# A decoder layer with product-key experts on one core: sines earlier, transposes later, expert weights in larger pieces

## The chip, the core and the metric

The kernel runs on 1 core of one Trainium2 chip. That core has TensorE (PE, matrix products into PSUM), VectorE (DVE), ScalarE (ACT), GpSimd (POOL) and SyncE (SP, which here only issues DMAs), and 16 DMA engines that all queues share. The metric is the device time of one execution in microseconds; of several executions the median is taken.

## The reference

One layer over 512 tokens of width 2048, everything in float32:

```python
h = rmsnorm(x, g_mix);  z = h @ w_in                 # 2048 x 4096: pool | q | k | v
x = x + concat(pool_mixer(z), dilated_attention(rope(q), rope(k), v)) @ w_out
x = x + cross_attention(rmsnorm(x), rmsnorm(mem))    # 4 heads, 256 memory tokens
x = x + peer_ffn(rmsnorm(x))                         # see below
out = rmsnorm(x, g_final)

def peer_ffn(h, w_pq, sub_keys_1, sub_keys_2, w_u, w_v):
    # 8 heads: top 16 of 128 keys in each of two halves, then top 16 of their sums
    # -> per token 128 experts out of 16384, with softmax gates
    a = einsum('td,tkd->tk', h, w_u[experts])        # w_u: 16384 x 2048
    return einsum('tk,tkd->td', gates * gelu(a), w_v[experts])
```

## The kernel before

**Tokens.** The 512 tokens are treated in three sets. The first 128 (T0) run ahead of the rest through the whole layer, and their experts are *gathered*: for each of the 128 experts of a token one row of `w_u` (8 KB) is read by an indirect DMA that POOL issues, DVE takes the dot product (`dot0`, L318), and later the same with rows of `w_v` (`axpy0`, L331). One such step moves 128 rows, 1 MB. The next 64 tokens (NS) do the same later (`dot1` L1075, `axpy1` L1086). The remaining 320 tokens (ND) run *dense*: all 16384 experts are multiplied, and gates that are zero for unchosen experts pick the result.

**Exactness.** Products run in the fast float32r form, so each weight tile of 128 x 1024 is split into a high part `wh` (ACT, L143) and a low part `wl` (raw minus high, on DVE or POOL, L144), and each product takes three matmuls (L150 to L152: wh by xh, wh by xl, wl by xh). `load_w` loads a tile (4 KB per partition, 512 KB in all) on SP into a ring of four tiles `wraw`, and splits it into one of three `wh`/`wl` buffers. `lo_eng` says who makes the low part.

**Stages, by the span of the profiled execution.** 0 to 380 us: T0's mixer, attention, cross attention and expert query (`ep` block, matmuls of L399 to L401). 380 to 730: the other 384 tokens' input projection (`z_chunk`, 48 matmuls each) with their attention; the routing of T0 (`pick_steps`: L274, L293, L295, L242 to L246) runs on DVE at the start of it. 730 to 890: output projection. 890 to 1000: cross attention. 1000 to 1140: expert query and its top 16 (`score`). 1140 to 1300: three times, for each block of 128 tokens, `pick` on DVE finds the experts, and three PE transposes (L1054 to L1056) turn the two key indices and the gate; beside it PE computes the first `w_u` chunks (`a_chunk`, 48 matmuls, two weight tiles), seven per block (KB = 7). 1300 to 1690: chunks 21 to 55, with `gates` beside them (L1114, L1116 on DVE, L1119 on PE), which write the dense gates to DRAM; these 56 chunk results are parked in DRAM (`gad`). 1690 to 2700: the mixed stage: 8 groups of 16 `w_v` tiles (`dd`), with the next group's chunk of `w_u` after every even `dd`, so that PE's order of tiles is v, u, u, v, v, u, u, v. 2700 to 3090: `w_v` tiles alone; the chunk results come back from `gad`. Then the final norm.

**What sets the order.** The Python order gives priorities; a planner at build time then orders each engine's instructions by its own simulated timeline, except where an engine is under `manual_schedule`. On the chip every engine works strictly in that order: an instruction that waits holds all behind it. The gathered steps stand in one list, `queue`; `behind(rate)` takes steps off it between matmuls, and `issue_after` keeps each step behind the last low part that DVE made. `RATE` gives the steps per chunk in the stages: z (first three heads' pool chunks differ), output, cross, 1000 to 1300, and 1300 to 1690. In the mixed stage the rate follows from what is left in the list.

The first rope of the second token set needs `sinT` and `cosT`, made by `trig` (L229 to L239) from the positions, which ACT's queue loads at L762.

Of the kernel before, what the change touches and what calls it, by code (L numbers as in the profile page):

```python
# [9 lines left out]
F32 = mybir.dt.float32  # L10
# [24 lines left out]
NS = 64  # L35
SG = P // NS
NK = P // SG
# [3 lines left out]
WRAW = 4  # L41


RATE = (3.0, 2.2, 2.5, 2.0, 0.25, 1.2)
# [19 lines left out]
def hybrid_kernel(ctx: ExitStack, tc: tile.TileContext, a: dict, out: bass.AP):  # L64
# [52 lines left out]
    ring = [None, 0]  # L117

    def load_w2(src):
# [4 lines left out]
        if raw is None:  # L124
            raw = wp.tile([P, 1024], F32, name="wraw", bufs=WRAW)
# [7 lines left out]
    anchor = [None]  # L133

    def load_w(src, lo_eng=None, parts=1):
        raw = wp.tile([P, 1024], F32, name="wraw", bufs=WRAW)
        wh = wp.tile([P, 1024], F32R, name="wh")
        wl = wp.tile([P, 1024], F32R, name="wl")
# [9 lines left out]

    def mm3(ps, wh, wl, xh, xl, start, stop):
# [215 lines left out]
    halo = kt.tile([P, 8, 16], F32, name="halo")  # L365

# [8 lines left out]
    with tc.tile_pool(name="ep", bufs=1) as ep, tc.manual_schedule(engines={mybir.EngineType.SP}):  # L375
# [48 lines left out]
        def mem_in(t):  # L424
            raw = wp.tile([P, 4, MEM], F32, name="wraw", bufs=WRAW)
# [327 lines left out]
    with tc.tile_pool(name="ac", bufs=1, reuse_waits="tile") as ac, tc.tile_pool(name="at", bufs=2, reuse_waits="tile") as at:  # L753
# [116 lines left out]
    with tc.tile_pool(name="xt", bufs=2, reuse_waits="tile") as xt:  # L870
# [78 lines left out]
        for t in range(8):  # L949
            w = load_w(a["w_co"][t], G if t % 2 else V) if t >= 1 else None  # L950
            for e in range(2):
# [9 lines left out]
                sumsq(xtmp, accx, xT[:, c, :], c == 0, TR)  # L961
# [52 lines left out]
    hy = ctx.enter_context(tc.tile_pool(name="hy", bufs=1, side="right", reuse_waits="tile"))  # L1014
# [22 lines left out]
    with tc.tile_pool(name="tw", bufs=1, reuse_waits="tile") as tw:  # L1037
        for b in range(RB):
# [276 lines left out]
```

## Time and profile before

| | |
|---|---|
| time, 3 runs | 3184.94 us median (3177.57 to 3185.37) |
| profiled execution | 3175.37 us, its span 3173.6 us |
| busy | PE 93%, DVE 76%, POOL 45%, ACT 41% of the span |
| granted TensorE clock | 0.968 of full on average |
| DMA | 912.79 MB, 288 GB/s over the span |
| chain that ended last | PE 66%, DVE 20%, DMA 5%, issue 5% |

A busy share is an average over stages that have different limits; the stage table among the rows below shows PE's busy time in each. The granted clock is in parts of full speed: 1.00 is 2.4 GHz and 0.50 is 1.2 GHz; a value between them is a stretch that had both. A wait row reads: who waited, for whom, total us, times, longest.

### The profile page before, as it was taken

How to read it: one execution, taken by the hardware profiler on the slowest of the kernel's cores; microseconds unless marked ns; L12 is line 12 of the kernel's file. 1: busy time of each engine (PE TensorE's matmuls, PEld its weight loads, DVE VectorE, ACT ScalarE, POOL GpSimd, SP SyncE). 2: the span in 40 equal slices, each digit the busy share in tenths (PEclk: the TensorE clock that was granted, in tenths of full speed). 3: DMA queues.
4: the chain of work that ended last, by engine and by line, in shares of the span. 5: the costliest groups of instructions: out<-in, count | busy, mean ns of one | idle time of the engine just before them, and what ended most of it. 6: DMA issues, size and time to landing. Idle time of an engine off the chain costs nothing.

```text
span 3173.6 us, 47405 instructions
## 1 busy us (share of the span) xinstructions
PE 2947.7 (93%) x18311; PEld 2832.5 (89%) x18311; DVE 2422.7 (76%) x3360; ACT 1298.6 (41%) x1789; POOL 1433.8 (45%) x826
## 2 busy tenths in 40 slices
PE   7999879998988997899998999999999999999997
PEld 5868769988978997899998999999999999899997
DVE  7797877798878579599894767777777678787756
ACT  5676534432344443355543333333433333233334
POOL 0000046644534665544546555555555554454532
PEclk9999989999989998999999999999999999999998
DMA  7886737888975344588888989999899999999953
GB/s 261 295 300 214 244 119 282 330 309 339 342 266 192 111 127 124 182 302 318 315 304 315 357 325 359 357 367 355 330 372 353 353 354 358 346 357 362 343 163 106
DMA packets 243521, 912.79 MB, mean 288 GB/s; under 512 B 23488, under 2 KB 85600, under 8 KB 192224
## 3 DMA queue, kind: packets, MB, share of 16 engines
q1 hardware_dynamic: 136304, 471.21, 42.2%
q0 software_dynamic: 55296, 402.68, 32.1%
q10 hardware_dynamic: 51696, 35.88, 3.7%
q8 instruction: 144, 2.36, 0.3%
q14 instruction: 81, 0.66, 0.1%
HBM read 874.22 MB, written 35.45 MB: 287 GB/s over the span
## 4 chain that ended last, share of the span: by engine, by line
PE 66%; DVE 20%; DMA 5%; issue 5%; ACT 2%; POOL 0%; ACTq 0%; POOLq 0%; DVEq 0%; SPq 0%
PE pm L150 11%; PE pm L152 11%; PE pm L151 11%; PE pa L152 9%; PE pa L150 9%; PE pa L151 9%; DVE wl L144 2%; DVE u L1114 2%; DVE oh L295 1%; DVE oh L293 1%; PE pm L400 1%; PE pm L401 1%; PE pm L399 1%; PE pa L1119 1%; DMA rows<-in_w_v_rows_dram,sidx 1%
## 5 line engine op out<-in xcount | busy, mean ns | idle before, releaser
L144 POOL TENSOR_TENSOR wl<-wraw,wh 128x1024 fp32r<-128x1024 f32 x369 | 930.5, 2526 | 1433.3 <-ACT wh L143 1401.4
L143 ACT ACTIVATE wh<-wraw 128x1024 fp32r<-128x1024 f32 (+1 forms) x658 | 693.7, 1058 | 1042.1 <-PE pm L151 467.0
L152 PE MATMUL pa<-ch,wl 128*128 128x320 f32 x2048 | 634.5, 312 | 25.4 <-DVE wl L144 23.5
L150 PE MATMUL pm<-dH,wh 128*128 128x320 f32 x2048 | 640.4, 313 | 15.0 <-DVE cl L1164 6.5
L152 PE MATMUL pm<-dH,wl 128*128 128x320 f32 x2048 | 640.6, 313 | 6.1 <-DVE wl L144 3.9
L150 PE MATMUL pa<-ch,wh 128*128 128x320 f32 x2048 | 636.7, 311 | 7.3 <-DVE xT L1193 4.7
L151 PE MATMUL pm<-dL,wh 128*128 128x320 f32 x2048 | 639.0, 312 | 0.0
L151 PE MATMUL pa<-cl,wh 128*128 128x320 f32 x2048 | 635.3, 310 | 0.0
L144 DVE TENSOR_TENSOR wl<-wraw,wh 128x1024 fp32r<-128x1024 f32 (+1 forms) x289 | 377.4, 1308 | 166.5 <-ACT wh L143 158.7
L152 PEld LDWEIGHTS pa<-ch,wl 128*128 128x128 f32 x2048 | 387.1, 189 | 30.4 <-DVE wl L144 28.1
L150 PEld LDWEIGHTS pm<-dH,wh 128*128 128x128 f32 x2048 | 389.2, 190 | 16.3 <-DVE cl L1164 6.8
L150 PEld LDWEIGHTS pa<-ch,wh 128*128 128x128 f32 x2048 | 388.3, 190 | 10.2 <-ACT ch L1163 5.2
L152 PEld LDWEIGHTS pm<-dH,wl 128*128 128x128 f32 x2048 | 389.3, 190 | 8.2 <-DVE wl L144 5.4
L151 PEld LDWEIGHTS pm<-dL,wh 128*128 128x128 f32 x2048 | 389.3, 190 | 0.0
L151 PEld LDWEIGHTS pa<-cl,wh 128*128 128x128 f32 x2048 | 388.1, 190 | 0.0
L150 PE MATMUL pm<-hH,wh 128*128 128x384 f32 x1024 | 355.9, 348 | 10.4 <-DVE k L811 3.4
L152 PE MATMUL pm<-hH,wl 128*128 128x384 f32 x1024 | 354.2, 347 | 10.5 <-DVE wl L144 10.5
L151 PE MATMUL pm<-hL,wh 128*128 128x384 f32 x1024 | 354.4, 346 | 5.2 <-DVE hL L874 4.4
L1193 DVE TENSOR_TENSOR xT<-pa,xT 128x320 f32<-128x320 f32 x256 | 124.7, 487 | 196.6 <-PE pa L152 191.0
L150 PEld LDWEIGHTS pm<-hH,wh 128*128 128x128 f32 x1024 | 197.6, 193 | 17.1 <-issue 5.8
L152 PEld LDWEIGHTS pm<-hH,wl 128*128 128x128 f32 x1024 | 197.6, 193 | 13.4 <-DVE wl L144 12.5
L151 PEld LDWEIGHTS pm<-hL,wh 128*128 128x128 f32 x1024 | 197.7, 193 | 6.9 <-DVE hL L874 4.7
(413 smaller groups left out, 4571.6 us busy)
## 6 DMA issues: line engine op xcount, KB each, us to landing
wraw<-in_w_u_dram SPq DMA_DIRECT2D x256, 512.0 KB
wraw<-in_w_v_dram SPq DMA_DIRECT2D x256, 512.0 KB
wraw<-in_w_in_dram SPq DMA_DIRECT2D x64, 512.0 KB
xT<-in_w_in_f_dram SPq DMA_DIRECT2D x63, 512.0 KB
gd<-stage SPq DMA_DIRECT2D x10, 2048.0 KB
gt<-gd ACTq DMA_DIRECT2D x32, 640.0 KB
wraw<-in_w_pq_f_dram SPq DMA_DIRECT2D x32, 512.0 KB
wraw<-in_w_out_dram SPq DMA_DIRECT2D x32, 512.0 KB
```

The source lines that it names most:

```text
L143: S.activation(wh[:, c], raw[:, c], AF.Copy)
L144: i = (lo_eng or V).tensor_tensor(wl[:, c], raw[:, c], wh.bitcast(F32)[:, c], op=ALU.subtract)
L150: TE.matmul(ps, wh, xh, start=start, stop=False)
L151: TE.matmul(ps, wh, xl, start=False, stop=False)
L152: TE.matmul(ps, wl, xh, start=False, stop=stop)
L293: V.tensor_tensor(oh, iota50.unsqueeze(1).broadcast_to([P, 16, NCAND]), cf[:, h, :].unsqueeze(2).broadcast_to([P, 16, NCAND]), op=ALU.is_e ...
L295: V.tensor_tensor(oh, oh, ecand[:, h, :].unsqueeze(1).broadcast_to([P, 16, NCAND]), op=ALU.mult)
L399: TE.matmul(ps, xh, wh, start=start, stop=False)
L400: TE.matmul(ps, xh, wl, start=False, stop=False)
L401: TE.matmul(ps, xl, wh, start=False, stop=stop)
L1114: V.tensor_tensor(u, iota.unsqueeze(1).unsqueeze(1).broadcast_to([P, 2, 4, P]), e12T[:, :, t:t + 4].unsqueeze(3).broadcast_to([P, 2, 4, P] ...
L1193: V.tensor_tensor(xT[:, dd, NS:], ps[:, :ND], xT[:, dd, NS:], op=ALU.add)
```

## The change

1. `trig` for the second token set moves from the attention block into the block before (hooks of the expert query of T0); its tables are kept in `accx` and in a new `cosT`.
2. The three transposes after each `pick` stand behind the seven chunks of their block in the program, and `issue_after(last_mm)` keeps them behind the last matmul of those chunks.
3. In the mixed stage each `w_u` chunk's low parts go to POOL for the first tile and DVE for the second, where they went to one engine for both, changing from chunk to chunk. With `w_v`, whose even tiles go to DVE and odd ones to POOL, the two now take strict turns.
4. `w_u` and `w_v` are laid out so that one DMA brings two tiles, 8 KB per partition, 1 MB; `load_pair` puts them in a ring of three pairs: two in the old four tiles, the third in `xraw`, where the token rows `htok` lay. Those rows go to DRAM (`hyd`) and are read back when the 64 tokens' steps begin; their result stays in a row buffer.
5. `RATE` rises in the early stages and falls in the stage of 1300 to 1690 (1.2 to 0.95). The sum of squares beside the last cross projection adds on POOL. The 64 tokens' normed rows take one DVE instruction where they took two.

```diff
-RATE = (3.0, 2.2, 2.5, 2.0, 0.25, 1.2)
+RATE = (3.2, 2.4, 2.8, 2.5, 0.25, 0.95)
...
+    wraw = wp.tile([P, 4, 1024], F32, name="wraw", bufs=1)
+    slot = [0, 0]
+
+    def raw1():
+        slot[0] += 1
+        return wraw[:, slot[0] % 4]
+
+    def load_pair(src):
+        slot[1] += 1
+        i = slot[1] % 3
+        raw = xraw if i == 2 else wraw[:, 2 * i:2 * i + 2]
+        nc.sync.dma_start(raw, src)
+        return raw
...
-        TE.matmul(ps, wl, xh, start=False, stop=stop)
+        last_mm[0] = TE.matmul(ps, wl, xh, start=False, stop=stop)
...
-            V.tensor_tensor(acc, acc, q, op=ALU.add)
+            (eng or V).tensor_tensor(acc, acc, q, op=ALU.add)
...
+        def trig_rows():
+            V.tensor_copy(cosT, posr[0])
+            V.tensor_scalar(cosT, cosT, scalar1=invf, scalar2=None, op0=ALU.mult)
+            trig(cosT, ep.tile([P, TR], F32, name="jk", bufs=2)[:32], sinT, cosT)
+            V.tensor_scalar(sinT[0:16], sinT[0:16], scalar1=-1.0, scalar2=None, op0=ALU.mult)
+
+        hooks_x[2][0] = [pos_in]
+        hooks_x[2][5] = [trig_rows]
...
-        posi = tmp2k(TR, I32)[:32]
-        nc.scalar.dma_start(posi, a["positions"][:, T0:].broadcast_to([32, TR]))
-        ang = tmp2k()[:32]
-        V.tensor_copy(ang, posi)
-        V.tensor_scalar(ang, ang, scalar1=invf, scalar2=None, op0=ALU.mult)
-        trig(ang, tmp2k()[:32], sinT, cosT)
-        V.tensor_scalar(sinT[0:16], sinT[0:16], scalar1=-1.0, scalar2=None, op0=ALU.mult)
...
-                sumsq(xtmp, accx, xT[:, c, :], c == 0, TR)
+                sumsq(xtmp, accx, xT[:, c, :], c == 0, TR, eng=G)
...
-        lo = G if j < RB * KB else (V, G) if j < K1 else G if j < K1 + GRP or j % 2 == 0 else V
-        ps = proj_one(a["w_u"][j], dH, dL, ND, lo_eng=lo, rate=RATE[4] if j < RB * KB else RATE[5] if j < K1 else 0)
+        lo = G if j < RB * KB else (V, G) if j < K1 else G if j < K1 + GRP else (G, V)
+        ps = proj_one(None, dH, dL, ND, raw=load_pair(a["w_u"][j]), lo_eng=lo, rate=RATE[4] if j < RB * KB else RATE[5] if j < K1 else 0)
...
+            a_until(KB * b + KB)
             pt = pa.tile([P, 512], F32, name="pa")
-            TE.transpose(pt[:, 0:P], e12[:, 0, :], ident)
-            TE.transpose(pt[:, P:2 * P], e12[:, 1, :], ident)
-            TE.transpose(pt[:, 2 * P:3 * P], gtf, ident)
+            with tc.issue_after(last_mm[0].ins):
+                TE.transpose(pt[:, 0:P], e12[:, 0, :], ident)
+                TE.transpose(pt[:, P:2 * P], e12[:, 1, :], ident)
+                TE.transpose(pt[:, 2 * P:3 * P], gtf, ident)
...
-            a_until(KB * b + KB)
...
-    def start1():
+    def start1(s):
         gx[0] = gxp.tile([P, D], F32, name="gx")
-        S.copy(gx[0], hy1)
+        r = row_tile()
+        nc.sync.dma_start(r, hyd[s])
+        S.copy(gx[0], r)
...
-                wh, wl = load_w(a["w_v"][g, dd], lo_eng=G if dd % 2 else V)
+                if dd % 2 == 0:
+                    vraw = load_pair(a["w_v"][g, dd // 2])
+                wh, wl = load_w(None, lo_eng=G if dd % 2 else V, raw=vraw[:, dd % 2])
...
-    A["w_u"] = np.ascontiguousarray(i["w_u"][0].reshape(P, NCH, 2, 8, P).transpose(1, 2, 4, 3, 0)).reshape(NCH, 2, P, 1024)
+    A["w_u"] = np.ascontiguousarray(i["w_u"][0].reshape(P, NCH, 2, 8, P).transpose(1, 4, 2, 3, 0)).reshape(NCH, P, 2, 1024)
```

Three places show what the planner makes of it. ACT between the second and the third routing of a block (1252 to 1290 us before): `gT` is the copy that follows each group of transposes, `wh` a split weight tile, `ga` the result of one chunk. Before, from the second `gT` to the third:

```order
L1060 COPY gT<-pa 128x128
L301 ACT_TABLE_LOAD
L301 ACTIVATE gt<-gt 128x128
L143 ACTIVATE wh<-wraw 128x1024 x2
L1026 ACT_TABLE_LOAD
L1026 ACTIVATE ga<-pm 128x320
L143 ACTIVATE wh<-wraw 128x1024 x2
L1026 ACTIVATE ga<-pm 128x320
L143 ACTIVATE wh<-wraw 128x1024 x2
L1026 ACTIVATE ga<-pm 128x320
L143 ACTIVATE wh<-wraw 128x1024
L1060 COPY gT<-pa 128x128
```

Now, the last twelve rows up to the third `gT`:

```order
L160 ACTIVATE wh<-wraw 128x1024
L160 ACTIVATE wh<-xraw 128x1024
L1051 ACTIVATE ga<-pm 128x320
L160 ACTIVATE wh<-xraw 128x1024
L160 ACTIVATE wh<-wraw 128x1024
L1051 ACTIVATE ga<-pm 128x320
L160 ACTIVATE wh<-wraw 128x1024 x2
L1051 ACTIVATE ga<-pm 128x320
L160 ACTIVATE wh<-wraw 128x1024
L160 ACTIVATE wh<-xraw 128x1024
L1051 ACTIVATE ga<-pm 128x320
L1088 COPY gT<-pa 128x128
```

Three chunk results stood between the two copies, and seven do now (three of them above these rows). On PE the three groups of transposes stood behind 410, 578 and 761 of the chunks' matmuls, and stand behind 394, 672 and 1008.

DVE at the first head of the attention (386 to 392 us before): `k` is the first key, t2k the buffers of `trig` and of the rope's shuffle. Before, `trig` (L764 to L239) begins between the top-16 instructions:

```order
L811 TENSOR_TENSOR k<-ma,r2c 128x384
L245 MAX mb<-ma 128x8
L246 MAX_INDEX mb<-mb,ma 128x8
L764 CAST t2k<-t2k 32x384
L246 MAX_INDEX mb<-mb,ma 128x8
L244 MATCH_REPLACE ma<-mb,ma 128x128
L765 TENSOR_SCALAR t2k<-t2k,invf 32x384
L244 MATCH_REPLACE ma<-mb,ma 128x128
L245 MAX mb<-ma 128x8
L229 TENSOR_SCALAR t2k<-t2k 32x384
L773 STREAM_SHUFFLE t2k<-q 32x384
```

Now both shuffles of the rope follow the key at once:

```order
L835 TENSOR_TENSOR k<-ma,r2c 128x384
L264 MAX mb<-ma 128x8
L265 MAX_INDEX mb<-mb,ma 128x8
L797 STREAM_SHUFFLE t2k<-q 32x384
L797 STREAM_SHUFFLE t2k<-k 32x384
```

The instructions of `trig` are gone from here; the first of them now stands among the splits of T0's cross-attention input, 173 rows ahead of this `k`, and the last after the third group of T0's expert query.

SP in the mixed stage, with the engines whose semaphores each load waits for. Before, one row is one tile:

```order
L142 DMA wraw<-in_w_v_dram 128x1024 [waits DMAHW6_49,Pool_49]
L142 DMA wraw<-in_w_v_dram 128x1024 [waits DMAHW7_49,DVE_49]
L142 DMA wraw<-in_w_u_dram 128x1024 [waits DMAHW0_49,DVE_49]
L142 DMA wraw<-in_w_u_dram 128x1024 [waits DMAHW1_49,DVE_49]
L142 DMA wraw<-in_w_v_dram 128x1024 [waits DMAHW2_49,Pool_49]
```

Now one row is two tiles:

```order
L129 DMA wraw<-in_w_u_dram 128x2048 [waits DMAHW4_49,Pool_49]
L129 DMA wraw<-in_w_v_dram 128x2048 [waits DMAHW2_49,DVE_49,Pool_49]
L129 DMA xraw<-in_w_u_dram 128x2048 [waits DMAHW7_49,Pool_49]
L129 DMA xraw<-in_w_v_dram 128x2048 [waits DMAHW4_49,DVE_49,Pool_49]
L129 DMA wraw<-in_w_u_dram 128x2048 [waits DMAHW6_49,DMAHW1_49,Pool_49]
```

A `w_u` pair now waits for POOL's low part of the second tile of the `w_v` pair three loads back, whose place it takes; a `w_v` pair takes the place of a `w_u` pair.

## Rows read from the trace of the kernel before

**Rows 1.** The windows view, by stage; busy us (instructions) per engine, PEclk, DMA share, GB/s.
```profile
380.00:520.00 140.00, 117.66 (x627) 111.22 (x628) 102.19 (x262) 53.07 (x95) 64.76 (x45) 0.88 0.44 150
520.00:730.00 210.00, 195.22 (x1045) 182.62 (x1044) 178.86 (x228) 77.51 (x141) 118.22 (x87) 0.96 0.88 328
730.00:890.00 160.00, 150.19 (x821) 148.25 (x820) 130.35 (x138) 53.62 (x71) 81.98 (x53) 0.97 0.88 338
890.00:1000.00 110.00, 91.74 (x449) 81.59 (x448) 86.34 (x119) 53.73 (x104) 38.84 (x27) 0.91 0.63 230
1140.00:1300.00 160.00, 128.52 (x810) 126.03 (x809) 153.03 (x381) 52.09 (x67) 93.17 (x36) 0.88 0.39 123
1300.00:1690.00 390.00, 371.45 (x2626) 366.83 (x2625) 327.43 (x282) 187.02 (x209) 195.37 (x91) 0.98 0.82 301
1690.00:2700.00 1010.00, 992.17 (x6708) 989.54 (x6707) 720.03 (x689) 356.69 (x438) 545.19 (x326) 0.99 0.92 351
2700.00:3090.00 390.00, 366.07 (x2415) 359.63 (x2414) 285.48 (x299) 126.17 (x150) 183.21 (x104) 0.98 0.86 316
```

**Rows 2.** The waits view, PE, 380 to 520: total us, times, longest.
```profile
PE pa L818 <- POOL q L776: 13.3, 1, 13.3
```

**Rows 3.** The windows view in slices of 10 us, the first head.
```profile
400.00:410.00 10.00, 0.00 (x0) 0.00 (x0) 10.00 (x62) 3.16 (x4) 3.55 (x4) 0.68 0.10 30
410.00:420.00 10.00, 4.67 (x12) 2.78 (x12) 9.97 (x33) 0.83 (x2) 2.58 (x3) 0.50 0.11 43
```

**Rows 4.** The timeline of DVE, 375 to 420: start, us, [idle before <-releaser].
```profile
389.96 0.35 DVE L764 CAST t2k<-t2k 32x384 f32<-32x384 int32 x1 [2.95 <-DMA t2k<-in_positions_dram]
```

**Rows 5.** The waits view, PE, 1000 to 1300.
```profile
PE pa L1054 <- DVE e L1052: 20.8, 3, 11.0
```

**Rows 6.** One line, L1054: number, duration ns min/median/max, first and last start.
```profile
L1054 PE MATMUL pa<-ident,e x3: 448/474/476, 1212.4 to 1289.7; 128*128 128x128 f32 x3
```

**Rows 7.** The timeline of PE, 1238 to 1256.
```profile
1252.09 0.47 PE L1054 MATMUL pa<-ident,e 128*128 128x128 f32 x1 [10.96 <-DVE e L1052]
```

**Rows 8.** The windows view in slices of 20 us, after the third routing.
```profile
1300.00:1320.00 20.00, 20.00 (x138) 20.00 (x137) 0.00 (x0) 7.33 (x9) 14.51 (x7) 1.00 0.60 193
```

**Rows 9.** The windows view in slices of 100 us, one where PE never waits.
```profile
2000.00:2100.00 100.00, 100.00 (x684) 100.00 (x683) 70.24 (x61) 36.21 (x44) 55.59 (x34) 1.00 0.93 349
```

**Rows 10.** Groups by line, DVE: count, busy us, mean ns, idle before.
```profile
L318 DVE CUSTOM_DVE_ANT_0 rows<-rows,gx 128x2048 f32<-128x2048 f32 x66 | 150.0, 2276 | 6.4 <-DMA rows<-in_w_u_rows_dram,sidx 6.4
L225 DVE TENSOR_TENSOR accx<-accx,xtmp 128x384 f32<-128x384 f32 x30 | 19.8, 659 | 1.9 <-ACT xtmp L224 1.8
```

**Rows 11.** Groups by line, POOL and ACT (part 5 of the page for L144, L143).
```profile
L144 POOL TENSOR_TENSOR wl<-wraw,wh 128x1024 fp32r<-128x1024 f32 x369 | 930.5, 2526 | 1433.3 <-ACT wh L143 1401.4
L143 ACT ACTIVATE wh<-wraw 128x1024 fp32r<-128x1024 f32 (+1 forms) x658 | 693.7, 1058 | 1042.1 <-PE pm L151 467.0
L1003 POOL TENSOR_TENSOR qh<-xT,r2c 128x320 f32<-128x320 f32 x16 | 13.9, 879 | 0.0
```

**Rows 12.** DMA queues, 2105 to 2106 us: packets, MB, share of 16 engines.
```profile
q0 software_dynamic: 38, 0.29, 67.9%
q1 hardware_dynamic: 39, 0.13, 32.2%
```

**Rows 13.** DMA queues, 2285 to 2286 us, the rows of 8 KB read by ACT.
```profile
q10 hardware_dynamic: 49, 0.40, 100.8%
```

**Rows 14.** The timeline of SP, 2285 to 2310.
```profile
2293.60 1.42 SPq L142 DMA_DIRECT2D wraw<-in_w_v_dram  x2
```

**Rows 15.** The timeline of ACT, 2262 to 2312.
```profile
2305.35 1.06 ACT L143 ACTIVATE wh<-wraw 128x1024 fp32r<-128x1024 f32 x1 [4.53 <-DMA wraw<-in_w_v_dram]
```

**Rows 16.** The waits view, all engines, 1690 to 2700.
```profile
PE pa L152 <- DVE wl L144: 8.1, 4, 3.0
```

**Rows 17.** The waits view, all engines, 2700 to 3090.
```profile
PE pa L152 <- DVE wl L144: 15.4, 13, 2.3
ACT wh L143 <- DMA wraw<-in_w_v_dram: 16.2, 6, 4.5
```

More of the change, by code (lines that the diff above doesn't have):

```diff
@@ L34 @@
 RB = TR // P
-NS = 64
-SG = P // NS
-NK = P // SG
+SETS = ((0, 64),)
+NS = sum(n for _, n in SETS)
 ND = TR - NS
 NTB = ND // 32
-WRAW = 4
-RATE = (3.0, 2.2, 2.5, 2.0, 0.25, 1.2)
+RATE = (3.2, 2.4, 2.8, 2.5, 0.25, 0.95)
 PK, Z0 = 3, 1
@@ L133, in hybrid_kernel, with split_tiles, load_w @@
     anchor = [None]
[L135 to L138, printed above, removed]
+    def split_tiles():
+        return wp.tile([P, 1024], F32R, name="wh"), wp.tile([P, 1024], F32R, name="wl")
+    def load_w(src, lo_eng=None, parts=1, raw=None):
+        there = raw is not None
+        raw = raw if there else raw1()
+        wh, wl = split_tiles()
         n = 1024 // parts
@@ L141, in load_w @@
             c = slice(p_ * n, (p_ + 1) * n)
-            nc.sync.dma_start(raw[:, c], src[:, c])
+            if not there:
+                nc.sync.dma_start(raw[:, c], src[:, c])
             S.activation(wh[:, c], raw[:, c], AF.Copy)
@@ L1086, in axpy1, with end1 @@
         V.scalar_tensor_tensor(out=gx[0], in0=r, scalar=sact2[:, k:k + 1], in1=gx[0], op0=ALU.mult, op1=ALU.add)
-    def end1():
-        y1[0] = hy.tile([P, D], F32, name="htok")
-        S.copy(y1[0], gx[0])
-    queue += [start1] + [lambda k=k: dot1(k) for k in range(NK)] + [turn1] + [lambda k=k: axpy1(k) for k in range(NK)] + [end1]
-    with tc.tile_pool(name="gw", bufs=2, side="right", reuse_waits="tile") as gw:
+    def end1(s):
+        ys[s] = row_tile()
+        S.copy(ys[s], gx[0])
@@ L1095, in hybrid_kernel, with add1 @@
+    def add1(s):
+        o, n = SETS[s]
         for k4 in range(4):
             pt = pa.tile([P, 512], F32, name="pa")
-            for kk in range(4):
-                k = 4 * k4 + kk
-                hn = gw.tile([P, SG, NS], F32, name="hn0")
-                for g in range(SG):
-                    V.scalar_tensor_tensor(out=hn[:, g, :], in0=xT[:, k, :NS], scalar=gains[:, 3, k:k + 1], in1=r2c[:, :NS], op0=ALU.mult, op1=ALU.mult)
-                TE.transpose(pt[:, kk * P:(kk + 1) * P], hn.rearrange("p g t -> p (g t)"), ident)
@@ L1103, in hybrid_kernel @@
-            S.copy(hy1[:, k4 * 512:(k4 + 1) * 512], pt)
+            with tc.issue_after(last_mm[0].ins):
+                for kk in range(4):
+                    TE.transpose(pt[:, kk * P:(kk + 1) * P], ys[s][:, (4 * k4 + kk) * P:(4 * k4 + kk + 1) * P], ident)
+            x = xT[:, 4 * k4:4 * k4 + 4, o:o + n]
+            for g in range(P // n):
+                V.tensor_tensor(x, pt.rearrange("p (k g t) -> p k g t", k=4, t=n)[:, :, g, :], x, op=ALU.add)
+    for s, (o, n) in enumerate(SETS):
+        ks, at_ = range(o, o + n), len(queue) + 6
+        queue += [lambda s=s: start1(s)] + [lambda k=k: dot1(k) for k in ks] + [lambda c=slice(o, o + n): turn1(c)]
+        queue += [lambda k=k: axpy1(k) for k in ks] + [lambda s=s: end1(s)]
+        if s:
+            queue.insert(at_, lambda s=s - 1: add1(s))
@@ new lines, in hybrid_kernel @@
+    with tc.tile_pool(name="gw", bufs=2, side="right", reuse_waits="tile") as gw:
+        for s, (o, n) in enumerate(SETS):
+            for k4 in range(4):
+                pt = pa.tile([P, 512], F32, name="pa")
+                for kk in range(4):
+                    k = 4 * k4 + kk
+                    hn = gw.tile([P, P // n, n], F32, name="hn0")
+                    V.scalar_tensor_tensor(out=hn, in0=xT[:, k, o:o + n].unsqueeze(1).broadcast_to([P, P // n, n]), scalar=gains[:, 3, k:k + 1],
+                                           in1=r2c[:, o:o + n].unsqueeze(1).broadcast_to([P, P // n, n]), op0=ALU.mult, op1=ALU.mult)
+                    TE.transpose(pt[:, kk * P:(kk + 1) * P], hn.rearrange("p g t -> p (g t)"), ident)
+                hs4 = gw.tile([P, 512], F32, name="hs4")
+                S.copy(hs4, pt)
+                nc.scalar.dma_start(hyd[s, :, k4 * 512:(k4 + 1) * 512], hs4)
@@ L1203, in hybrid_kernel @@
                 behind(1000)
-                for k4 in range(4):
-                    pt = pa.tile([P, 512], F32, name="pa")
-                    for kk in range(4):
-                        TE.transpose(pt[:, kk * P:(kk + 1) * P], y1[0][:, (4 * k4 + kk) * P:(4 * k4 + kk + 1) * P], ident)
-                    o = xT[:, 4 * k4:4 * k4 + 4, :NS]
-                    for sg_ in range(SG):
-                        V.tensor_tensor(o, pt.rearrange("p (k g t) -> p k g t", k=4, t=NS)[:, :, sg_, :], o, op=ALU.add)
+                add1(len(SETS) - 1)
                 for k in range(KD):
```

51 lines of the change are left out of this document (29 added, 22 removed).

## The prediction

> **What bounds the kernel now.** I read the table by stage first [rows 1]. PE is the wall: in the mixed stage (1690 to 2700 us) it is busy 992 of 1010 us, and a slice in which it never waits holds 684 matmuls in 100 us, 0.146 us each [rows 9]. A tile of 24 matmuls therefore takes 3.5 us. So time can come only from PE's idle stretches and from the low clock behind them. The largest, as a share, lie at the first head (380 to 520: 22 us idle, clock 0.88) and in the routing (1140 to 1300: 31 us idle, clock 0.88, with DVE busy 153 of 160). Between 1300 and 1690 PE idles 19 us, in the last `w_v` stage 24, in the whole mixed stage 18 [rows 1]. The waits view then names what PE waits for: the rope's sines in one wait of 13.3 us [rows 2] and the routing's transposes in three waits of 20.8 us [rows 5]. Of the weights it names only low parts that come late, 8.1 and 15.4 us [rows 16, 17].
>
> **Early sines.** DVE's cast of the positions waited 2.95 us for the DMA and started at 389.96 [rows 4]; the rest of `trig` followed between top-16 steps, and PE stood from 398 to 412. Its next slices hold 0 and 4.67 us of work, at clock 0.68 and 0.50 [rows 2, 3]. With the tables made long before, rope can follow the key at once, and PE loses neither the 13.3 us nor all of the slow clock behind them. The wait that is next is DVE, which is full in both slices [rows 3]: T0's routing is still there, and the scores' softmax queues in it. At worst all 13.3 us return as that wait (gain 0); at best the idle and slow time of both slices goes (about 15 idle, 22 with the clock). I take 15 of gain, near the upper end, since the order now has both shuffles ahead of the routing's large steps. `trig` itself, about ten DVE instructions of at most 0.5 us and two of ACT, goes to a stretch in which DVE is busy but PE also waits: cost 0 to 6, I take 2.
>
> **Later transposes.** Before, PE reached them at 1212.4, 1252.1 and 1289.7 [rows 6, 7], behind 410, 578 and 761 chunk matmuls, and waited each time. DVE's routing sets these times and is not changed. Now they stand behind 394, 672 and 1008. From 1212.4 on, 278 matmuls take 41 us, to 1253: the second routing is ready. Then 336 take 49 us, to about 1303 with the transposes: the third has been ready for 13 us. Before, at 1303 PE had done 761 + 13.5/0.146, about 851. The difference of 157 matmuls is 23 us. POOL makes these low parts, 2.53 us per tile of 3.5 [rows 11], so it keeps up. Ends: 0 if DVE takes it all back in the gates behind, 31 (the whole idle). I take 23, because DVE lies idle from 1300 to 1320 [rows 8]: it waits for PE's chunk 21 there, and gets it earlier now.
>
> **Rates.** Steps moved forward: z 11 x 0.2 + 8 x 0.2 = 3.8, output 16 x 0.3 = 4.8, cross 4 x 0.5 = 2; taken from 1300 to 1690: 35 x 0.25, about 9. A step costs DVE 2.28 us [rows 10]. So DVE loses 20 us of work where it is busy 327 of 390, and gains 9, 11 and 5 us where it has 31, 30 and 24 idle [rows 1]. I cost the forward steps at a third, 8, and the relief at half, 11: gain 3. If every forward step stalls PE half its length, loss 13; if the relief is worth 12 and the rest is free, gain 12.
>
> **Small edits.** The sums of squares leave DVE (15 x 0.66 = 10 us) for POOL (879 ns for 320 columns, so about 1.05 us for 384, 16 us) [rows 10, 11]; POOL is busy 39 of 110 there [rows 1]. Gain 2, ends -5 and 5. The first `xraw` load waits until PE has read the last tile of the pool that it replaces, and SP's next loads wait behind it; chunk 0 covers it with 7 us. Cost 2, ends 0 and 5. The 64 tokens' steps begin with a 1 MB read of `hyd`, issued by SP a few loads ahead; if late, DVE and with it PE wait. Cost 2, ends 0 and 8.
>
> **The ring of three pairs.** Where `w_u` or `w_v` comes alone, the ring is deeper than four tiles: the sixteen microseconds of waits for `w_v` loads after 2700 [rows 17] should go. PE waits there for DVE's low parts, whose DVE work the change leaves; gain 5, ends -8 and 15. In the mixed stage it is the reverse. PE's order is v u u v, 14.0 us a turn. A `w_u` pair takes the place of the `w_v` pair before, whose second tile is split only after both `w_u` tiles of its turn. From the landing of one `w_u` pair: ACT copies 1.06 us, POOL makes its first low part, then that of the next odd `w_v` tile, 2.53 each [rows 11]; then SP may issue the next pair: 6.1 us, or about 7.2 if POOL issues a row gather in between. This leaves 6.8 to 7.9 us from issue to landing before the turn grows. What does 1 MB take? With the gathers active, both queues moved about equal packets, 38 and 39 in one microsecond, but 0.29 MB of rows of 8 KB against 0.13 MB of weights of 4 KB [rows 12]. The engines take turns by packet. A load that ACT issued in 8 KB pieces moved 49 packets with 0.40 MB [rows 13], so pieces of 8 KB stay whole, and the weights' share rises from a third to half: about 0.2 MB/us, 5 us, and 2.5 us where no gather runs. No row shows alone what comes ahead of the first packet and behind the last: I add an estimate of 1 to 3 us, since the 11.7 us [rows 14, 15] are more than 0.52 MB takes at 0.13. So 4 to 8 us, against 6.8 to 7.9: mostly in time, with nearly none of the old slack. The worst of before took about 11.7 us from issue to split [rows 14, 15]. Against it, strict turns end POOL's three low parts in a row, part of the 8.1 us [rows 16]. Ends: gain 8, or 64 turns (8 groups of 8) x 1.1 us = 70. I take a cost of 10, nearer the low end, since the steady rows give in-time loads.
>
> The Trainium skill, page DMA: Bandwidth & Descriptors, section Anatomy of one DMA, fits a DMA by 2.0 us plus its bytes over 436 GB/s: 4.4 us for 1 MB, and the ring would cost 0, the sum -42. The trace differs: half that size took 11.7 us at worst here [rows 14, 15], so I keep 10.
>
> **Sum.** -15 + 2 - 23 - 3 - 2 + 2 + 2 - 5 + 10 = -32 us, against the profiled execution's 3175.37 (span 3173.6): 3143. That execution lay 9.6 us under the median of the runs, 3184.94, and I put the same sum on the median: 3153.
>
> **Rivals.**
> *The pairs come late (slower).* If the first-served rows and the start of each load keep a `w_u` pair 8 us or more on the way, each mixed turn grows. At 1.0 us a turn it costs 64; the other terms give -42, so +22: 3207. It decides from 0.66 us a turn. For it: the 11.7 us [rows 14, 15] and DMA at 0.92 busy [rows 1]. Against: equal packets [rows 12] and slack where no gather runs. It would be sure if the 8 KB pieces went as two packets of 4 KB: the share stays a third, 1 MB takes 1/0.14 = 7.1 us plus 1 to 3, and 0.2 to 3 us a turn are lost. The Trainium skill, same page, section SWDGE vs HWDGE vs iDMA, says that a packet is preferably at most 4096 B; by this rule that would happen, but the trace disagrees, with 49 packets for 0.40 MB [rows 13].
> *The routing's gain is given back.* If DVE's gates end no earlier, the 23 us return as PE's wait on them: -9, 3176. For it: DVE's 327 of 390 [rows 1]. Against: its idle slice [rows 8].
> *Everything gains.* Ring -4 instead of +10, last stage -12, rates -9: -59, 3126. For it: PE's waits on late low parts [rows 16, 17]; against: DVE's load is unchanged there.
>
> **Chances.** The forecast 0.47 (its own range 3130 to 3176), late pairs 0.20, gain given back 0.19, everything gains 0.14. The three runs spread by 8 us, and 0.3% (9.6 us) is what a measurement can tell from no change: faster means below 3175, slower above 3194. Faster: 0.44 + 0.14 + 0.07 = 0.65. Same: 0.03 + 0.04 + 0.10 = 0.17. Slower: 0.16 + 0.02 = 0.18. The range from 3115 to 3200 leaves out the worse half of the late pairs and the best of the last case.
>
> **What would show it.** In the new profile: PE's wait on POOL's rope at the first head under 3 us, and no empty slice there; transposes 15 us earlier by the sines, the first at about 1197 with its wait, the third at about 1288 with none; 1690 reached some 40 us earlier; the mixed stage 1010 to 1030 us long, with ACT waiting for `w_u` loads more than for `w_v`; `w_v` waits gone after it. Wrong, if the mixed stage is longer by over 40 us (late pairs), or if the start of the mixed stage moves by less than 20 us.

## The result and the profile after

The changed kernel takes 3420.21 us (3415.48 to 3425.57), the one before 3181.26 beside it: ratio 1.0752, 95% interval 1.0725 to 1.0779. It is slower by some 239 us, where 28 to 32 us of gain were forecast, and lies 220 us above the range. Where the time went is read first from the stages. Two rows of the view by line give marks: the first and the last start of the `w_u` products (`pm<-dH`) and of the `w_v` products (`pa<-ch`). Before:

```profile
L150 PE MATMUL pm<-dH,wh x2048: 304/309/636, 1136.8 to 2653.4; 128*128 128x320 f32 x187
L150 PE MATMUL pa<-ch,wh x2048: 304/308/607, 1740.9 to 3150.7; 128*128 128x320 f32 x187
```

After:

```profile
L169 PE MATMUL pm<-dH,wh x2048: 305/309/636, 1150.2 to 2862.6; 128*128 128x320 f32 x187
L169 PE MATMUL pa<-ch,wh x2048: 307/310/636, 1738.7 to 3391.1; 128*128 128x320 f32 x187
```

From these, four stages: up to the first chunk 1136.8 us before, 1150.2 after (+13); chunks 0 to 55 took 604.1, now 588.5 (-16); the mixed stage 912.5, now 1123.9 (**+211**); the last stage 497.3, now 528.5 (+31). The windows view of the profile after has in the same stretches as [rows 1]:

```profile
380.00:520.00 140.00, 123.04 (x669) 116.29 (x669) 110.25 (x259) 52.94 (x96) 75.62 (x52) 0.90 0.49 176
1140.00:1300.00 160.00, 129.17 (x831) 126.40 (x830) 152.96 (x409) 54.84 (x73) 98.53 (x39) 0.91 0.39 130
1300.00:1690.00 390.00, 376.42 (x2689) 372.40 (x2687) 320.29 (x260) 187.75 (x213) 191.56 (x83) 1.00 0.78 286
1690.00:2700.00 1010.00, 886.70 (x5554) 855.32 (x5555) 650.55 (x539) 291.52 (x362) 483.33 (x270) 0.95 0.73 286
2700.00:3090.00 390.00, 344.19 (x2159) 332.37 (x2158) 275.23 (x281) 113.12 (x142) 177.29 (x103) 0.95 0.82 312
```

From 1690 to 2700 PE had 6708 matmuls and now has 5554; the clock fell from 0.99 to 0.95, and the DMA engines are busy 0.73 where they were 0.92. So over the stage bandwidth is not what is short. Between the marks of the mixed stage PE is busy 982 us for some 6120 matmuls, before 903 for as many, and waits 142 us, before 9: of the 211 us, 133 are waits and 78 busy time, with the clock at 0.95 where it was 0.99. What PE waits for there, 1690 to 2862:

```profile
PE pm L169 <- ACT wh L160: 51.4, 38, 3.3
PE pa L169 <- ACT wh L160: 43.2, 34, 1.3
PE pm L171 <- POOL wl L161: 41.4, 29, 1.9
PE pm L169 <- DVE cl L1212: 7.7, 1, 7.7
```

High parts are late, where [rows 16] had only low parts, and ACT makes them late because it waits for `w_u` loads. The loop stands in one turn. SP, the issues of pairs:

```profile
2090.70 0.33 SPq L129 DMA_DIRECT2D wraw<-in_w_v_dram  x1
2095.16 0.33 SPq L129 DMA_DIRECT2D wraw<-in_w_u_dram  x1
2109.17 0.33 SPq L129 DMA_DIRECT2D wraw<-in_w_v_dram  x1
2112.36 0.33 SPq L129 DMA_DIRECT2D xraw<-in_w_u_dram  x1
```

ACT, the high parts of the same turn (a bracket gives the idle time before and its releaser):

```profile
2104.52 2.00 ACT L160 ACTIVATE wh<-wraw 128x1024 fp32r<-128x1024 f32 x2 [6.45 <-DMA wraw<-in_w_u_dram]
2106.43 1.04 ACT L160 ACTIVATE wh<-xraw 128x1024 fp32r<-128x1024 f32 x1
2122.57 2.01 ACT L160 ACTIVATE wh<-xraw 128x1024 fp32r<-128x1024 f32 x2 [1.03 <-DMA xraw<-in_w_u_dram]
```

POOL, from the landing of that `w_u` pair to the release of the next place:

```profile
2105.65 2.36 POOL L161 TENSOR_TENSOR wl<-wraw,wh 128x1024 fp32r<-128x1024 f32 x1 [8.60 <-ACT wh L160]
2108.16 1.75 POOL L114 DMA_INDIRECT rows<-in_w_v_rows_dram,sidx  x1 [0.15 <-issue]
2109.94 2.39 POOL L161 TENSOR_TENSOR wl<-xraw,wh 128x1024 fp32r<-128x1024 f32 x1
```

The pair issued at 2095.16 lands at 2104.52. High part, low part, a row gather and the low part of the second `w_v` tile take until 2112.33, 7.8 us; at 2112.36 SP issues the next `w_u` pair, and it lands at 2122.57, 10.2 us later. Over the some 60 turns in which ACT waited for the load, landing to next issue has a mean of 8.3 us (7.9 where POOL issues one row gather in that time, 9.1 where it issues two) and issue to landing one of 9.3; together 17.6, and a turn takes 1123.9/64 = 17.6 where it took 14.3. SP has mostly issued a `w_v` pair 3 to 4.5 us ahead of the `w_u` pair, here at 2090.70 and 2109.17. From the issue at 2095.16 to the landing at 2104.52 the queues (q0 the gathers, q1 the loads of SP) moved:

```profile
q0 software_dynamic: 387, 2.91, 73.6%
q1 hardware_dynamic: 146, 1.06, 26.9%
```

The 1.06 MB are the `w_u` pair itself: the `w_v` pair had moved its bytes by then, and the gathers moved 2.91 MB beside it. Summed in this way over the turns, the gathers move 2.4 MB on average between issue and landing, and the `w_v` pair 0.25 MB. Counted back from the landing by the pair's own bytes, the 9.3 us are 3.3 up to its first packets, 4.6 while it moves, and 1.4 from there to its use. The first half of the prediction's reading stands (packets stay whole, half of the bytes [rows 12, 13]): 1 MB in 4.6 us is about its 0.2 MB/us. What stands ahead of the first packet and behind the last took longer than it said.

### The profile page after: what moved, and what is told of

Read it like the earlier page. It is cut to its first block, busy times and chain, and to the rows that moved or that the text cites. A ratio compares the mean times of both kernels' runs of the same rounds, so it can differ in the third digit from the quotient of the medians.

```text
span 3413.7 us, 46891 instructions
## 1 busy us (share of the span) xinstructions
PE 3026.6 (89%) x18311; PEld 2869.6 (84%) x18311; DVE 2518.2 (74%) x3329; ACT 1292.8 (38%) x1790; POOL 1490.6 (44%) x841
## 3 DMA queue, kind: packets, MB, share of 16 engines
q8 instruction: 144, 2.36, 0.3%
## 5 line engine op out<-in xcount | busy, mean ns | idle before, releaser
L161 POOL TENSOR_TENSOR wl<-wraw,wh 128x1024 fp32r<-128x1024 f32 x275 | 691.3, 2516 | 1235.8 <-ACT wh L160 1175.3
L160 ACT ACTIVATE wh<-wraw 128x1024 fp32r<-128x1024 f32 (+1 forms) x488 | 506.7, 1054 | 913.1 <-PE pm L170 310.7
L169 PE MATMUL pm<-dH,wh 128*128 128x320 f32 x2048 | 662.0, 323 | 85.7 <-ACT wh L160 64.7
L171 PE MATMUL pm<-dH,wl 128*128 128x320 f32 x2048 | 662.5, 324 | 52.3 <-POOL wl L161 48.8
L170 PE MATMUL pm<-dL,wh 128*128 128x320 f32 x2048 | 655.5, 320 | 1.0 <-DVE dL L236 1.0
L169 PEld LDWEIGHTS pm<-dH,wh 128*128 128x128 f32 x2048 | 405.2, 198 | 98.7 <-ACT wh L160 80.7
L161 DVE TENSOR_TENSOR wl<-wraw,wh 128x1024 fp32r<-128x1024 f32 (+1 forms) x213 | 335.5, 1575 | 187.4 <-ACT wh L160 184.1
L170 PEld LDWEIGHTS pm<-dL,wh 128*128 128x128 f32 x2048 | 404.0, 197 | 1.3 <-DVE dL L236 1.2
L161 POOL TENSOR_TENSOR wl<-xraw,wh 128x1024 fp32r<-128x1024 f32 x94 | 238.3, 2537 | 318.7 <-ACT wh L160 307.6
L160 ACT ACTIVATE wh<-xraw 128x1024 fp32r<-128x1024 f32 x170 | 176.9, 1055 | 303.6 <-DMA xraw<-in_w_u_dram 87.4
```

What stands on the lines that cost most here:

```text
L171: last_mm[0] = TE.matmul(ps, wl, xh, start=False, stop=stop)
```

## The experiments

e1 to e4, e8, e13 and e14 are edits of the kernel after, e5 to e7 and e9 to e12 of the kernel before. Stages in us by the marks above (in the order u u v v, marked *, the border between mixed and last shifts, so only their sum compares); ratios to the kernel before, run on the same chip, with 95% intervals. Each stage is of one execution. Of an edit only the deciding lines are shown, some shortened and with comments added.

| kernel | to 1st chunk | chunks | mixed | last | median | ratio |
|---|---|---|---|---|---|---|
| before | 1136.8 | 604.1 | 912.5 | 497.3 | 3175 to 3182 | |
| after | 1150.2 | 588.5 | 1123.9 | 528.5 | 3420.21 | 1.0752 (1.0725 to 1.0779) |
| e1 tiles | 1154.1 | 597.7 | 934.3 | 524.2 | 3232.15 | 1.0150 (1.0111 to 1.0189) |
| e2 no turns | 1151.4 | 587.3 | 1056.6 | 525.1 | 3344.99 | 1.0531 (1.0490 to 1.0573) |
| e3 u u v v | 1148.0 | 595.7 | 902.7* | 540.9* | 3214.04 | 1.0112 (1.0080 to 1.0144) |
| e4 four pairs | 1149.3 | 585.6 | 944.2 | 537.7 | 3239.71 | 1.0190 (1.0154 to 1.0225) |
| e5 rates | 1148.6 | 591.8 | 939.5 | 517.2 | 3225.50 | 1.0151 (1.0136 to 1.0165) |
| e6 transposes | 1134.5 | 596.6 | 913.4 | 504.2 | 3164.19 | 0.9959 (0.9943 to 0.9974) |
| e7 sines | 1116.5 | 606.0 | 910.4 | 503.0 | 3164.54 | 0.9968 (0.9952 to 0.9984) |
| e8 u u v v, old rates | 1128.2 | 608.9 | 910.6* | 519.2* | 3191.29 | 1.0041 (1.0026 to 1.0057) |
| e9 sines, transposes | 1121.3 | 598.4 | 912.2 | 497.5 | 3151.68 | 0.9922 (0.9903 to 0.9941) |
| e10 last rate | 1136.7 | 592.6 | 936.2 | 512.9 | 3203.25 | 1.0086 (1.0066 to 1.0106) |
| e11 early rates | 1150.7 | 586.8 | 927.3 | 494.5 | 3184.18 | 1.0025 (1.0011 to 1.0040) |
| e12 strict turns | 1135.2 | 605.8 | 940.9 | 522.9 | 3225.97 | 1.0149 (1.0127 to 1.0172) |
| e13 w_u first | 1148.9 | 587.6 | 990.6 | 537.1 | 3291.12 | 1.0355 (1.0334 to 1.0376) |
| e14 w_u first, plain | 1131.5 | 608.2 | 948.2 | 524.8 | 3237.39 | 1.0188 (1.0159 to 1.0217) |

**The ring of pairs.** e1 releases tile by tile:

```diff
-        i = slot[1] % 3
-        raw = xraw if i == 2 else wraw[:, 2 * i:2 * i + 2]
+        i = slot[1] % 6          # one tile, 512 KB, per DMA
+        raw = xraw[:, i - 4] if i > 3 else wraw[:, i]
```

> The kernel after, with the same memory and the same DRAM layout, but as a ring of six single tiles: each tile is loaded by its own DMA (4 KB per partition, 512 KB) when its own slot is free. Theory L (the turn is a loop: a w_u pair may be issued only after POOL's low part of the second w_v tile of the turn before, and then lies about 10 us behind the w_v pair issued 3 us ahead of it): the turn falls from 17.5 to 14.0-14.3 us, total 3190 to 3225 us. Theory P (1 MB pieces of 8 KB are slow in themselves): the same here, 3190 to 3225. Theory T (the strict turns hold POOL): no change of the turn, 3390 to 3440.

e2 undoes the strict turns:

```diff
-G if j < K1 + GRP else (G, V)
+G if j < K1 + GRP or j % 2 == 0 else V
```

> The kernel after, with the strict turns undone: in the mixed stage a w_u chunk's two low parts go to one engine, changing from chunk to chunk. Theory T (POOL's two low parts and a gather in a row delay the release of the place): the turn falls by 2 us or more, total 3200 to 3300. Theory L: on POOL's chunks the loop grows by one low part of 2.5 us, on DVE's it shrinks by as much, mean the same, total 3380 to 3440. Theory P: 3400 to 3440.

e3 puts the chunk ahead of the even tile:

```diff
                 if dd % 2 == 0:
+                    if not last:
+                        nxt.append(c_chunk(GRP * order[i + 1] + dd // 2))
                     vraw = load_pair(a["w_v"][g, dd // 2])
...
-                if dd % 2 == 0 and not last:
-                    nxt.append(c_chunk(GRP * order[i + 1] + dd // 2))
```

> The kernel after, with pairs and their ring as they are, but PE's order in the mixed stage u u v v instead of v u u v (the chunk stands ahead of the even w_v tile), so that places come free in the order in which they were filled. Theory L: the released place has a whole pair of 7 us in reserve, the turn falls to 14.0-14.6 us, total 3190 to 3240. Theory P: the loads stay late, 3350 to 3430. Theory T: 3380 to 3440.

e4 has a fourth pair:

```diff
-        i = slot[1] % 3
+        i = slot[1] % 4          # i == 3: xraw2, in the place of rowx
```

> The kernel after, with a ring of four pairs, the fourth in the place of one of the four buffers of the gathered rows. Theory L: a w_u pair takes the place of a w_u pair, which is free half a turn earlier; the turn falls to 14.0-14.5 us, total 3190 to 3240, a little lost to the missing row buffer. Theory P: 1 MB pieces are late whatever the ring, 3350 to 3430. Theory T: 3380 to 3440.

e1, e3 and e4 bring the mixed stage back to 903 to 944 us, with pieces of 8 KB in two of them: the pieces are not slow in themselves (P falls), and the release is what binds (L). e1 came 7 us over its range and e4 to the edge of its own, for the losses below. e2 hit neither range. Between successive chunk activations on ACT a turn now took about 15 and 18 us by turns: when DVE makes both low parts, POOL has one to make between landing and next issue, which takes 5.7 to 8.2 us; when POOL makes both, it has three, and that takes 9.3 to 10.7. So the strict turns cost 67 us of the mixed stage in this ring: with them no turn is of the quicker kind, each takes 7.8 to 9.1.

e13 changes only which load SP issues first:

```diff
+        if behind_u and u_load:           # w_v pairs
+            with tc.issue_after(u_load[-1]):
+                nc.sync.dma_start(raw, src)
+        else:
+            u_load.append(nc.sync.dma_start(raw, src).ins)
```

> The kernel after, with one change of SP's order: the load of the next w_v pair is issued behind the load of the w_u pair, where it was issued about 3 us ahead of it. Ring, pairs, PE's order and strict turns stay. Theory U (the w_u pair, which the loop waits for, takes 10 us because 1 MB of w_v that is needed 20 us later goes ahead of it in the same queue): issue to landing falls to 5-7 us, the loop to 13-14.5, a turn to 14.1-14.8 us, the total to 3205-3245 us. Theory H (any 1 MB load takes 10 us beside the gathers): the turn stays above 16.5 us, total 3380 or more.

SP's issues of one turn of e13:

```profile
2099.74 0.33 SPq L135 DMA_DIRECT2D wraw<-in_w_u_dram  x1
2100.17 0.37 SPq L133 DMA_DIRECT2D wraw<-in_w_v_dram  x1
```

and ACT's first high part of that `w_u` pair:

```profile
2104.69 1.06 ACT L166 ACTIVATE wh<-wraw 128x1024 fp32r<-128x1024 f32 x1 [0.22 <-DMA wraw<-in_w_u_dram]
```

Here the pair lands 5.0 us after its issue, and between the two the queues moved:

```profile
q1 hardware_dynamic: 171, 1.27, 67.3%
q0 software_dynamic: 102, 0.70, 34.1%
```

Over the some 50 turns in which ACT waited for it, issue to landing has a mean of 7.1 us, where it was 9.3, with 1.3 MB of gathers in that time, where it had 2.4. Landing to next issue takes 8.5, where it took 8.3. The mixed stage fell by 133 of the 211 us and a turn to 15.5. H falls. U's order counts, but the gain was less than expected (a turn of 14.1 to 14.8; the total is 46 us over U's range), and its reason is not what the queues show: in the kernel after only 0.25 MB of the `w_v` pair still stood ahead of the `w_u` pair. In the turn shown there, the `w_v` pair moved first, from 2091 to 2095, then gathers alone up to 2098.7, and only then the `w_u` pair, beside gathers. So my reading is that an early `w_v` pair pushes the gathers into the time of the `w_u` load; that this is the whole path of the 133 us is not shown. The Trainium skill, page DMA: Bandwidth & Descriptors, section Queues, rings and completion order, says that an engine goes round between queues packet by packet; the trace agrees where both queues move, with 54 and 53 packets from 2117 to 2119 in the kernel after. From 2114 to 2115 q0 moved 51 and q1 none, although the `w_u` pair had been issued at 2112.36; why its first packets come so late stays open.

e14 is e13 with the RATE of before and without strict turns:

> The same order of SP's loads, with the RATE of before and without the strict turns: early sines, later transposes and pairs are what is left of the change. Theory U with the prices found so far (sines -12, transposes -12, pairs in time 0 to +15): 3155 to 3175 us. Theory H: 3280 or more. If the first pair loads cost what the kernel after shows at the first chunk (waits of 13 and 9 us): 3170 to 3190.

It came out 47 us above 3190, the end of its two lower ranges, and 43 under theory H's 3280. Against e9, which has the same sines and transposes with the old ring, it loses 0.0266 of the time, about 85 us: 10 ahead of the first chunk, where no pair is loaded yet and the small edits and the new buffers differ, 10 in the chunks, 36 in the mixed and 27 in the last stage. e8, below, has pairs in the order u u v v and loses 0.0119, about 38 us. Pairs in this memory are a loss in every order tried.

**The rates.** e5 is the kernel before with the new `RATE` alone, e10 with only its last value, e11 with only the first four:

```diff
-RATE = (3.0, 2.2, 2.5, 2.0, 0.25, 1.2)
+RATE = (3.2, 2.4, 2.8, 2.5, 0.25, 0.95)   # e5
+RATE = (3.0, 2.2, 2.5, 2.0, 0.25, 0.95)   # e10
+RATE = (3.2, 2.4, 2.8, 2.5, 0.25, 1.2)    # e11
```

> The kernel before with the new RATE alone. The prediction gave it -3 us (3178 on a median of 3181). Theory R (the 13 us that the kernel after loses ahead of the first expert chunk come from the steps moved forward, which fill DVE): that chunk starts 8 to 15 us later, chunks 21 to 55 give back 5 to 10, total 0 to +10 us. Rival Q (the loss is of the sines' new order on DVE): no change ahead of the chunk, total -10 to 0.

> The kernel before with only RATE's last value lowered, 1.2 to 0.95. Theory F (a rate costs where it shifts the phase of the steps against the turns, so that two steps and the products of a chunk stand on DVE between a high part and its low part: five stalls of 5.47 us in the mixed stage with all new rates): nothing changes ahead of the first chunk, 8 to 12 us gained up to the first mixed tile, and the mixed and last stages lose 20 to 45, total 3190 to 3215. Rival N (the loss is of the number of steps moved forward alone): total 3165 to 3172.

> The kernel before with only the first four values of RATE raised. Theory F: the first chunk 12 us later, as with all new rates, and behind it a loss or none according to the phase, 0 to 40 us, total 3185 to 3225. Rival N: the forward steps also cost later, all of the 49 us, total 3215 to 3230.

e5 lost 49 us, far outside both theories: 12 ahead of the first chunk, 12 won back in the chunks, and 27 and 20 in the two stages behind them, although the gathers there are as many (165 and 61, before 167 and 59). In the mixed stage PE's waits add up to 29 us, before 9; five of e5's are of up to 5.5 us, 27.4 together. One of them, on PE:

```profile
1887.15 0.64 PE L152 MATMUL pa<-ch,wl 128*128 128x320 f32 x1 [5.47 <-DVE wl L144]
```

and what DVE did ahead of it:

```profile
1878.36 0.50 DVE L1159 TENSOR_TENSOR pm<-pm,gt 128x320 f32<-128x320 f32 x1 [2.35 <-ACT pm L1026]
1878.77 2.35 DVE L331 SCALAR_TENSOR_TENSOR gx<-rows,sact,gx 128x2048 f32<-128x2048 f32 x1
1881.02 0.48 DVE L1164 TENSOR_TENSOR cl<-pm,ch 128x320 fp32r<-128x320 f32 x1
1881.43 0.49 DVE L1193 TENSOR_TENSOR xT<-pa,xT 128x320 f32<-128x320 f32 x1
1881.84 2.35 DVE L331 SCALAR_TENSOR_TENSOR gx<-x,sact,gx 128x2048 f32<-128x2048 f32 x1
1884.09 3.01 DVE L144 TENSOR_TENSOR wl<-wraw,wh 128x1024 fp32r<-128x1024 f32 x1
```

Two gathered steps of 2.35 us stand ahead of a low part that PE needs at once. My reading is that the planner put them there because the list is at another phase when the mixed stage begins; no run shows this by itself. e10 loses in the same stages with nothing changed ahead of the chunks: it won 11.5 us in them, as forecast, and lost 24 and 16 behind. e11 lost 14 ahead of the first chunk, and 15 in the mixed stage, and won 17 in the chunks; its total lies 1 us under F's range and 31 under N's. F holds on the stages; that every loss is a 5.47 us stall doesn't, since e10's waits there are of 3.3 us at most.

**Sines and transposes.** e6, e7 and e9 are the kernel before with the parts 2, 1, and both, of the change as the diff has them.

> The kernel before with the later transposes alone. The prediction's step: -23 us, 3150 to 3165, from the first chunk to the first mixed w_v tile 604 us before, now 580. Rival G (DVE's gates take it back): -3 to 0 us, the same 604.

> The kernel before with the early sines alone. The prediction's step: -13 us, the first expert chunk 10 to 16 us earlier than 1137. Theory Q (the waited-for sines only become a wait on DVE, with both shuffles ahead of T0's routing and the softmax behind it): 0 to +13 us, the first chunk at 1137 to 1150.

> The kernel before with the early sines and the later transposes together, nothing else. If the two gains (each about 12 us alone) lie in different stages and add: 3148 to 3156 us on a median of 3177, a ratio of 0.992. If the time behind the routing takes one of them back: 3160 to 3168.

Each gains 10 to 13 us, and they add: e9 beats both kernels, 0.9922. With e7 the first chunk came 20 us earlier, more than the 10 to 16 expected, and the last stage gave 6 back; in e9, which is the same up to there but for the planner's order, it came 15.5 earlier. e6 came in its range for the time, but the chunks took 596.6 where 580 was expected. In the kernel after the three transposes run at 1227.6 to 1338.0 and idle for 0.4 us together. Their row by line:

```profile
L1082 PE MATMUL pa<-ident,e x3: 272/333/415, 1227.6 to 1338.0; 128*128 128x128 f32 x3
```

But PE now waits at two other places between 1140 and 1300:

```profile
1220.57 0.63 PE L169 MATMUL pm<-dH,wh 128*128 128x320 f32 x1 [8.66 <-ACT ga L1051]
1294.85 0.63 PE L169 MATMUL pm<-dH,wh 128*128 128x320 f32 x1 [13.29 <-ACT wh L160]
```

and ACT ahead of the first of them:

```profile
1218.55 0.47 ACTq L1069 DMA_DIRECT2D idd<-ei  x1
1219.14 1.06 ACT L160 ACTIVATE wh<-wraw 128x1024 fp32r<-128x1024 f32 x1 [16.77 <-DVE indf L287]
```

ACT stands 16.8 us for DVE's routing, because a DMA that ACT's queue issues from its result is ahead of the next high part. In the kernel before ACT stood at the same place too, for 10.75 us. Ahead of the second, longer wait it is no DMA: there ACT has the copy `gT` of the second group of transposes, and DVE the copy of their other part:

```profile
1291.96 0.27 ACT L1088 COPY gT<-pa 128x128 f32<-128x128 f32 x1 [20.31 <-DVE e12T L1087]
1291.52 0.41 DVE L1087 COPY e12T<-pa 128x256 f32<-128x256 f32 x1
```

PE had made these transposes at 1270.4 to 1271.0, but DVE first went on with the next block's routing, and ACT waited for DVE's copy with the next high parts behind it. These two waits of PE are 22 us, as much as the 20.8 that went [rows 5]. e6, which has the old ring, waits 13.4 us for high parts in its chunks too, so it isn't the pairs. What is left of the gain is the wait for the gates, 14.7 us before from 1300 to 1742, 5.0 after.

**Strict turns, and the rest.** e12 is the kernel before with the line of e2's diff the other way round.

> The kernel before (ring of four single tiles) with the strict turns alone. With the ring of three pairs they cost 75 us, because POOL made two low parts in a row ahead of the release and both engines' low parts fell together. Theory L: without pairs a place is released tile by tile, so the mixed stage stays within 15 us of its 912, total 3165 to 3195. Rival T (strict turns cost by themselves, whatever the ring): 3225 to 3260.

It lost 51 us, so my theory's range fell and the rival's held. Half of it is in the last stage, which the edit doesn't touch: there too the order is another. e8 is e3 with the RATE of before:

> The kernel after with the order u u v v in the mixed stage, and the RATE of before. Theory R: the first chunk comes 8 to 13 us earlier than in the same kernel with the new RATE (1148.0), total 3200 to 3210. Rival Q: no earlier, total 3212 to 3225. For the last stage (w_v alone, 30 us longer than before in all variants so far): if the steps' distribution is its cause, it falls to 500-510 us, else it stays at 525-540.

It gained 23 us on e3, more than either range, 20 of them ahead of the first chunk; mixed and last stage together stayed 20 us over before, so that the rates are not the only loss of the two.

## Why the prediction was wrong

**The step that failed: the ring of three pairs in the mixed stage.** It stood with +10 us, ends -8 and 70; the stage lost 211, 3.3 us a turn. The loop was right in kind, and both of its parts were too small. The chain from landing to the next issue was put at 6.1 us, or 7.2 with a row gather in between, and took a mean of 8.3: every turn had a gather there, a third of them two. The load was put at 4 to 8 us and took 9.3: its bytes moved in 4.6, as forecast, but what comes ahead of the first packet and behind the last, an estimate of 1 to 3 us, took 4.7, and 1.1 MB of gathers moved ahead of the pair's first packets. I costed a pair as if it were issued by itself. The planner issues the next `w_v` pair, whose place comes free first, ahead of the `w_u` pair that PE needs first; my rows of SP's order show both, but I read from them only which place each takes, not which is needed when. e13 puts 133 us on that order. What it leaves is about what the other parts cost alone in the mixed stage: rates 27 (e5), strict turns 28 (e12), pairs in the better order 36 (e14); with 133 that is 224, near the 211. The totals of the parts do not add like that, since a turn that waits for its load hides other waits. The two figures that the prediction takes from the Trainium skill, page DMA: Bandwidth & Descriptors, sections Anatomy of one DMA and SWDGE vs HWDGE vs iDMA, stand there for DMAs that GpSimd issues: the fit behind its estimate of 4.4 us, and the 4096 B of a packet. The pairs are issued on SP.

**The rival** of late pairs named first-served rows and the start of each load, which is what the queues show, its place and its point of decision, 0.66 us a turn, and gave it 0.20; but at 1.0 us a turn, and 3.3 were lost. The slow end of the term's range was drawn from the same sizes. The prediction's second sign of being wrong came as well: the mixed stage starts only 2 us earlier (1738.7, before 1740.9), since the new rates took back ahead of the chunks what the sines gave (e11 +14, e7 -20), and ACT's waits took most of what the transposes gave.

**Rates**: -3 forecast, with ends -12 and 13; +49 alone. The steps ahead of the first chunk cost 12, a little over my 8, and the relief behind it was 12, near my 11. What failed is the tacit assumption that stages with as many steps as before keep their time: the planner ordered them anew.

**Early sines**: -13 with their cost, measured -12 by the medians and -10 by the ratio 0.9968. PE's wait on POOL is gone, as forecast, and the wait that is next is DVE, as the bound said: 5.0 us before, and in the waits view after, 380 to 520:

```profile
PE pa L842 <- DVE t2k L846: 14.1, 2, 7.4
```

**Later transposes**: -23, measured -13 (e6). The wait at the transposes is gone, as said, but the next wait was misnamed: I looked at DVE and POOL, and it was ACT, held by a DMA issue and by the copy `gT` that both wait for DVE.

**The last stage**: -5, measured +31. The waits for `w_v` loads went, as forecast; the low parts of DVE came later instead, where [rows 17] had 15.4 us. The waits view of PE after, 2863 to 3391:

```profile
PE pa L171 <- DVE wl L161: 28.3, 16, 3.5
```

That this stage grew by 16 us in e10 and by 26 in e12, whose edits lie elsewhere, shows that it does not hang on its own code alone: the planner's order differs there too, and which rows of that order do it stays open. The sums of squares, the first `xraw` load and the `hyd` read were not tried alone. Ahead of the first chunk e14 and e8 came 10 and 7 us later than e9 with the same rates and sines, so that the forecast gain of 2 for the sums of squares is not borne out; e7 and e9 differ there by 5, though.

## What to carry to other kernels

A ring of few large pieces is priced by its whole loop: from landing through every instruction up to the release, and then from the issue to the landing with everything that the DMA engines have to move by then, gathers issued beside the release and loads that are needed later but whose place comes free first. Where a planner orders engines, a small number that sets a rate moves work in all later stages; it has to be timed by itself, since equal counts per stage don't make equal times. When a wait is moved away, look on every engine that does something with the late result, the DMA issues and copies of ACT among them: the next wait can sit behind those.

## What the runs showed of the hardware

DVE's low parts of the mixed stage took a median of 1.23 us before and 2.10 after, with the same shape, while POOL's kept 2.4:

```profile
L161 DVE TENSOR_TENSOR wl<-wraw,wh x85: 1211/2096/2580, 1739.9 to 2854.3; 128x1024 fp32r<-128x1024 f32 x85
```

In the turn shown above POOL begins one at 2105.65 for 2.36 us and DVE one at 2106.55, which takes 2.54. By the timelines, 75 of DVE's 127 low parts in this stage take over 1.5 us. Of these, 74 start while POOL makes a low part, and each ends 1.1 us after POOL's: DVE waits until POOL is done. Those with no low part of POOL beside them take 1.22. Without the strict turns (e2), or in the order u u v v (e3), the median is 1.22; it is 1.23 in e12 and e13 too, which have strict turns, but 25 and 48 of their 128 take over 1.5 us in the same way. The Trainium skill, page SBUF — State Buffer, section Who interferes with whom, says that a DVE instruction with two inputs in SBUF contends with a GpSimd instruction that reads SBUF; the trace agrees, with DVE as the one that is late.
